# A decoder layer with attention and a state scan: the far groups' values by Strassen's scheme, with x's sums made by adding transfers, an earlier scan, and quad operands issued ahead of reads

## Chip, cores and metric

The kernel runs on one core of one Trainium2 chip. The time is that of the device for one execution, in microseconds (us): the median of three runs. A profile of one further execution shows what each engine did: PE is TensorE (matmuls), PEld its weight loads, DVE VectorE, ACT ScalarE, POOL GpSimd, SP SyncE. POOL and SP do little but issue DMA transfers.

## The reference, cut to what matters

One layer on x of 512 tokens by 1024 channels, in float32:

```python
proj = x @ w_in            # q | k | v (3 dilation groups x 8 heads x 64 each) | u (512) | gate logits (2 x 1024)
q, k = apply_rope(q, pos), apply_rope(k, pos)
for g, (window, dilation) in enumerate(((128, 1), (512, 4), (2048, 16))):
    o_g, lse_g = dilated_group_attention(q[:, :, g], k[:, :, g], v[:, :, g], window, dilation)
...
y_attn = attn @ w_attn_br                       # the groups' outputs weighted by softmax of lse
y_s = s5_ssm(u, ...)                            # complex diagonal state scan: h' = a h + b u, y = Re(c h) + d u
glu = gelu(y_s) @ w_glu
y_ssm = (glu[..., :512] * sigmoid(glu[..., 512:])) @ w_ssm_br
mixed = gates[..., 0, :] * y_attn + gates[..., 1, :] * y_ssm
h = layer_norm(alpha * x + mixed @ w_out)
x = layer_norm(alpha * h + (silu(h @ w_ff_gate) * (h @ w_ff_up)) @ w_ff_down)
```

The change concerns v of the groups 1 and 2 (the "far" values, 512 tokens by 2 x 512 columns, over 1024 channels), and the order of the scan's and the attention's work around it.

## The kernel before

**Precision.** Every float32 factor is held as a high part, rounded to the format that the matmul takes, and a low part, the rest. A product is three matmuls (high by high, low by high, high by low), accumulated in PSUM.

**Weights.** The 128 x 2048 blocks of `w_in` are fetched by SP, 1 MB each (two raw buffers). Each is split in two halves of 128 x 1024: ACT casts the high part (line 201), DVE subtracts it from the raw weights to get the low part (line 202). The parts go to one of three slots (class `Weights`). When a step's matmuls have been issued, `release` gives its slot back and issues the next split.

**Steps.** The list STEPS (line 35) gives the stages of the projection. A step is 24 matmuls of 128 x 128 by 512 tokens (lines 208 to 210), that is 8 pieces of 128 channels with 3 matmuls each. The steps are u (0 to 3), v of group 0 (4 to 7), gate logits (8 to 19), k of group 0 (20 to 23), q of group 0 (24 to 27), and the far values (28 to 35, `pv`). From step 36 on come five quads: the far q and k pairs (`QUADS` 0 to 3) and the last gate logits. A quad is a 2 x 2 block product by Strassen's scheme: seven products, each of 24 matmuls of 256 columns (line 1148), on sums of weight blocks (made by DVE in place, tile `rq`) and sums of x. `prepare_quad` issues sums, cast and subtraction for a product's operand; `quad_evict` reads the banks x, y and z when a product has completed what they hold: ACT copies into `qsnap` (line 1181), DVE adds and applies the rotation. Behind the quads follow the GLU, the branch projections, the output projection and the feed-forward part, which the change leaves as they are except for the order of PSUM banks.

**x's sums.** Strassen's x operands (`x23`, `x4` and one overwriting a quarter of `x_hi`, `x_lo`) are made from x in another order of tokens, fetched by POOL (`xf`, 2 x 1 MB). DVE makes four sums (`sums_x`), ACT and DVE split them (`split_x`). All this lies at steps 30.6 to 34.2.

**The order around them.** Each engine takes its instructions strictly in the order in which they were issued. All other work is placed by a table written by hand: `at_step(n, f)` runs f when the steps have come to n; a whole or half number is the middle or the end of a step, quads count four steps each. The state scan is dealt out by `drip`, so many columns of elementwise operations each half step, to DVE (line 79). Its matmuls of y (`ssm_out`, lines 718 and 726) come in two rounds in the middle of the steps 28 and 29, each followed at once by ACT's copies out of `yt` (line 734), DVE's additions of `yc`, and the GELU. `turn_y` (step 30) turns the result by way of DRAM. SCORES and WEIGHTS place the attention of the far groups: scores (`s`, line 827), with masks and sums on DVE (line 838), and transposes of the weights (`t`, line 850).

Of the kernel before, what the change touches and what calls it, by code (L numbers as in the profile page):

```python
# [16 lines left out]
P = 128  # L17
# [81 lines left out]
class Weights:  # L99
# [65 lines left out]

    def release(self):
        slot = self.held.popleft()
        if slot[0] is None and not self.extra_ok():
            return
        self.free.append(slot)  # L170
        self.split()


def emit(ctx, tc, i, out):
# [530 lines left out]
    def ssm_out(rnd):  # L705

        if rnd == 0:
            late.take(1000)
            ssm["ysb"] = gat(0, "ysb").rearrange("p (a i b c) -> p a i b c", a=2, i=4, b=2)
        ut, h, y = ssm["ut"], ssm["h"], ssm["ysb"]  # L710
        tb, cb = ([ring_(f"y{n}{rnd}{e}").rearrange("p (o i c) -> p o i c", o=2, i=2) for e in range(2)]
                  for ring_, n in ((scores, "t"), (turned, "c")))
        for e in range(2):
            for par in range(2):
                for half, rows in halves64:
                    for x, cols in halves64:
                        i_ = 4 * rnd + 2 * e + x
                        pe.matmul(tb[half][cols, par, e], ssm["tm"][rows, 2 * i_ + par, :], ut[rows, 2 * i_ + par, :],
                                  start=True, stop=True)
        for e in range(2):  # L720
            for half in range(2):
                for r in range(2):
                    for par, rows in halves64:
                        for x, cols in halves64:
                            i_ = 4 * rnd + 2 * e + x
                            pe.matmul(cb[par][cols, half, e], caf[rows, i_, r, half, :], h[r][rows, 2 * i_ + half, :],
                                      start=(r == 0), stop=(r == 1))
        is_ = slice(2 * rnd, 2 * rnd + 2)
        yf = [y[:, half, is_].rearrange("p i b c -> p (i b c)") for half in range(2)]
        y2 = at.tile([P, 2, 512], F32, tag=("sw", "cq")[rnd], name=f"y2_{rnd}", bufs=1)  # L730
        y2 = [y2[:, half] for half in range(2)]
        for half in range(2):
            for par in range(2):
                act.copy(y[:, half, is_, par], tb[half][:, par])
# [119 lines left out]
    def attn_values(kind, hp):  # L854
# [148 lines left out]
    at_step(9.5, store_k)  # L1003
    for j in range(4):
# [1 line left out]
    at_step(13, blocks)  # L1006
    at_step(13, states)
    for rnd in range(2):
        at_step(28 + rnd, ssm_out, rnd)
    at_step(30, turn_y)  # L1010
    for kind in range(2):
        for j, n in enumerate(SCORES[kind]):
            if j > 0:
# [46 lines left out]
                6: [t23[n][:, 4:8] for n in range(2)], 7: [t23[n][:, 0:4] for n in range(2)]}  # L1060

    def fetch_x():
        for n, h in enumerate(("g0", 2)):
            forms_x[n] = home(h, f"xf{n}").rearrange("p (k t) -> p k t", k=KT)
            pool.dma_start(forms_x[n], i["xk"][n].rearrange("p (k t) -> p k t", k=KT))

    def sums_x(n):
        strassen_sums(forms_x[0], forms_x[1], n)

    def split_x(n):  # L1070
        h1, h2 = forms_x[0], forms_x[1]
        if n == 0:
            t23 = [home(h, f"x23{m}", F32R).rearrange("p (k t) -> p k t", k=KT) for h, m in ((5, "h"), (7, "l"))]
            t4 = home(8, "x4", F32R).rearrange("p (n k t) -> p n k t", n=2, k=4)
            forms_x["f"] = forms_of(xp, t23, [t4[:, m] for m in range(2)])
        hi, lo = forms_x["f"][(7, 6, 4, 5)[n]]
        split(hi, lo, (h2[:, 0:4], h2[:, 4:8], h1[:, 4:8], h1[:, 0:4])[n])

    at_step(30.6, fetch_x)
    for n in range(4):  # L1080
        at_step(32 + 0.4 * n, sums_x, n)
        at_step(33 + 0.4 * n, split_x, n)


    qr, qops, qbank, qsnap, qz = {}, {}, {}, {}, {}
# [40 lines left out]

        w.after = rest

    w.jobs[quad_first] = deque((lambda j=j, n=n: prepare_quad(j, n)) for j in range(len(QUADS)) for n in QPREP)
    w.loads[quad_first] = deque((lambda b=b: load_quad(0, b)) for b in (0, 2))  # L1130
    qnext = deque(j for j in range(len(QUADS)) for n in QORDER)
    X_HOMES = ("g0", "g0", 1, 4, 4)

    def quad_bank(j, key):
        return bank({"x": 2 * (j % 2), "y": 2 - 2 * (j % 2), "z": 1}[key], f"q{key}{j}")

    def quad_product(j, n):
        key = {1: "x", 6: "x", 7: "x", 4: "x", 2: "y", 5: "z", 3: "z"}[n]
# [776 lines left out]
```

## Time and profile before

| | us |
|---|---|
| median of 3 runs (823.75 to 824.73) | 824.17 |
| the profiled execution | 825.21 |
| its span, first to last instruction | 823.4 |
| steps 28 to 35 with two y rounds and the first far scores (165.97 to 219.68) | 53.71 |
| the five quads and the attention between them (219.68 to 357.23) | 137.55 |
| from there to the tail | 446.27 |

The profile records every instruction of one execution. "Busy" is the time in which an engine ran at least one. Matmuls overlap in the records: how fast they follow each other is seen in their starts, not in their lengths. A bracket behind a row gives how long the engine idled before it, and which instruction or transfer released it. The window rows that the prediction shows give the busy time of each engine in one stretch of the span, with the granted clock of PE (1.00 is full speed). In nearly the whole span PE is busy; its idle time in the stages above is below 2 us each.

### The profile page before, as it was taken

The page shows a single profiled execution, that of the slowest core. Times are in us where ns is not written, and L with a number is a line of the kernel's source. Part 1 is how long each engine was busy: PE and PEld are TensorE (multiplying, and loading weights), DVE is VectorE, ACT ScalarE, POOL GpSimd, SP SyncE. Part 2 cuts the span into 40 slices and gives each one's busy share as a digit, 9 for nine tenths or more (in the row PEclk, how much of TensorE's full clock was granted, in tenths as well). Part 3 has the DMA queues.
Part 4 walks back from the last instruction along what each step waited for, and adds up shares of the span by engine and source line. Part 5 has one row for each costly group of instructions (what it writes and reads, how often), then busy time and mean ns, then how long its engine had stood idle before and what let it go on. Part 6 is the DMA issues. An engine that isn't in the chain of part 4 may idle for free.

```text
span 823.4 us, 13781 instructions
## 1 busy us (share of the span) xinstructions
PE 810.5 (98%) x5608; PEld 726.7 (88%) x5608; DVE 653.4 (79%) x1043; ACT 402.7 (49%) x597; POOL 76.3 (9%) x94
## 2 busy tenths in 40 slices
PE   9999999999999999999999999999999999999995
PEld 7888888888899999988888899999999999888884
DVE  6985899663888889755986699877777789789986
ACT  5964321245557625775333246555555545555520
POOL 0000001310002331100000320000000000020104
PEclk9999999999999999999999999999999999999998
DMA  8733435756226635652615134333323333674453
GB/s 338 189 113 127 159 139 145 154 129 205 78 78 140 138 91 122 181 216 93 252 55 205 51 123 169 119 107 106 106 109 112 115 111 111 273 168 149 147 132 102
DMA packets 31471, 116.43 MB, mean 141 GB/s; under 512 B 7600, under 2 KB 12464, under 8 KB 21680
## 3 DMA queue, kind: packets, MB, share of 16 engines
q1 hardware_dynamic: 23808, 91.83, 32.2%
q0 software_dynamic: 5968, 22.02, 12.4%
q10 hardware_dynamic: 1632, 1.70, 0.6%
q8 instruction: 44, 0.72, 0.3%
q14 instruction: 19, 0.16, 0.1%
HBM read 99.55 MB, written 9.70 MB: 133 GB/s over the span
## 4 chain that ended last, share of the span: by engine, by line
PE 92%; DVE 3%; DMA 1%; ACT 1%; POOL 1%; issue 1%; DVEq 0%; SPq 0%; ACTq 0%
PE qx L1148 5%; PE dnx L1672 5%; PE dnz L1672 4%; PE pg L208 3%; PE pg L209 3%; PE pg L210 3%; PE pv L208 3%; PE qz L1148 2%; PE pv L209 2%; PE pv L210 2%; PE pu L607 2%; PE dny L1672 2%; PE qy L1148 2%; PE wo L210 2%; PE wo L209 2%; PE b L210 2%
## 5 line engine op out<-in xcount | busy, mean ns | idle before, releaser
L202 DVE TENSOR_TENSOR wlo<-raw,whi 128x1024 fp32r<-128x1024 f32 x52 | 63.8, 1231 | 32.0 <-ACT whi L201 32.0
L201 ACT CAST whi<-raw 128x1024 fp32r<-128x1024 f32 x52 | 54.2, 1046 | 41.4 <-PE pq L209 17.5
L1472 ACT CAST whi<-sums 128x1024 fp32r<-128x1024 f32 x40 | 42.0, 1049 | 66.2 <-DVE sums L342 66.2
L1119 ACT CAST whi_q<-rq 128x1024 fp32r<-128x1024 f32 x28 | 29.2, 1051 | 42.1 <-DVE rq L342 42.1
L342 DVE TENSOR_TENSOR wlo<-sums,whi 128x1024 fp32r<-128x1024 f32 x40 | 48.8, 1220 | 0.0
L342 DVE TENSOR_TENSOR wlo_q<-rq,whi_q 128x1024 fp32r<-128x1024 f32 x28 | 34.1, 1222 | 12.9 <-ACT whi_q L1119 12.8
L1672 PE MATMUL dnx<-whi_d,pc 128*128 128x512 f32 (+1 forms) x128 | 38.2, 376 | 0.0
L208 PE MATMUL pg<-x_hi,whi 128*128 128x512 f32 x96 | 37.6, 392 | 0.0
L209 PE MATMUL pg<-x_lo,whi 128*128 128x512 f32 x96 | 37.4, 389 | 0.0
L840 ACT ACTIVATE un<-un,st 128x256 f32<-128x256 f32 (+1 forms) x64 | 30.8, 483 | 13.4 <-DVE st L838 13.4
L210 PE MATMUL pg<-x_hi,wlo 128*128 128x512 f32 x96 | 37.4, 389 | 0.0
L765 POOL DMA_DIRECT2D kq<-qz x32 | 25.2, 1315 | 108.9 <-PE s L827 48.1
L955 ACT ACTIVATE gt<-pg,bgate 128x512 f32<-128x512 f32 x12 | 8.3, 690 | 42.5 <-PE pg L210 42.5
L1584 ACT CAST whi_d<-dn 128x1024 fp32r<-128x1024 f32 x16 | 16.9, 1053 | 22.8 <-DVE dn L342 10.8
L1672 PEld LDWEIGHTS dnx<-whi_d,pc 128*128 128x128 f32 x128 | 23.6, 188 | 4.4
L208 PE MATMUL pv<-whi,x_hi 128*128 128x512 f32 x64 | 25.4, 397 | 0.0
L209 PE MATMUL pv<-wlo,x_hi 128*128 128x512 f32 x64 | 25.0, 390 | 0.0
L210 PE MATMUL pv<-whi,x_lo 128*128 128x512 f32 x64 | 24.9, 389 | 0.0
L342 DVE TENSOR_TENSOR wlo<-ra,whi 128x1024 fp32r<-128x1024 f32 x20 | 24.4, 1220 | 0.4 <-ACT whi L1472 0.4
L1594 POOL DMA_DIRECT2D whi_db<-in_w_dp x3 | 1.7, 576 | 246.1 <-PE dny L1672 242.4
L1672 PE MATMUL dnx<-wlo_d,pc 128*128 128x512 f32 (+1 forms) x64 | 24.1, 376 | 0.0
L1148 PE MATMUL qx<-x23h,whi_q 128*128 128x256 f32 x80 | 23.2, 290 | 0.7 <-ACT qsnap L1181 0.7
(800 smaller groups left out, 2939.2 us busy)
## 6 DMA issues: line engine op xcount, KB each, us to landing
raw<-in_w_in SPq DMA_DIRECT2D x16, 1024.0 KB, 4.9
ra<-in_w_gu SPq DMA_DIRECT2D x10, 1024.0 KB, 4.7
rb<-in_w_gu SPq DMA_DIRECT2D x10, 1024.0 KB, 4.9
rq<-in_w_quad SPq DMA_DIRECT2D x16, 512.0 KB, 4.0
dn<-in_w_dq SPq DMA_DIRECT2D x8, 1024.0 KB, 4.8
kq<-qz POOLq DMA_DIRECT2D x32, 128.0 KB, 5.4
raw<-in_w_br SPq DMA_DIRECT2D x4, 1024.0 KB, 4.7
raw<-in_w_out SPq DMA_DIRECT2D x4, 1024.0 KB, 4.8
```

The source lines that it names most:

```text
L201: act.copy(hi, src)
L202: dve.tensor_tensor(lo, src, hi.bitcast(F32), op=ALU.subtract)
L208: pe.matmul(dst, a[0], b[0], start=first, stop=False)
L209: pe.matmul(dst, a[0], b[1], start=False, stop=False)
L210: pe.matmul(dst, a[1], b[0], start=False, stop=last)
L342: eng.tensor_tensor(o, a, b, op=op)
L765: pool.dma_start(dst[32 * q : 32 * q + 32], z[32 * (q ^ 1) : 32 * (q ^ 1) + 32], accum_op=ALU.add)
L840: act.activation(pt, pt, AF.Exp, bias=mneg, scale=-1.0, accum_out=zsum)
L1119: act.copy(hi, src)
L1148: pe.matmul(d[:, 256 * e : 256 * e + 256], p_[:, e, k, :], q_[:, k, :], start=(first and e == k == m == 0), stop=(k == 3 and m == 2), skip ...
L1472: act.copy(hi, src)
L1672: pe.matmul(acc[key][0 if key == "v" else e][:, cs], p_, q_[:, cs], start=(key, e) not in begun, stop=(m == 2), skip_group_check=True)
```

## The change

**Far values.** The eight steps become one 2 x 2 block product (two halves of tokens; two halves of the 1024 channels; group 1 and group 2 columns) in seven products by Strassen's scheme. Each has two halves u of 12 matmuls with 512 columns. x's operands are stationary here and the weights stream. Three pairs of banks accumulate: x (0, 7), y (1, 2), z (5, 6). Product 4 starts banks 0 and 7 afresh, after products 1, 6 and 7 have been read out.

```diff
-STEPS += [("v", _g, _un, _c) for _g in (1, 2) for _un in range(2) for _c in range(2)]
+    VORDER = (1, 2, 5, 6, 3, 7, 4)
...
+    def prepare_v():
+        n, u = vleft.popleft()
+        a11, a12, a21, a22 = (vraw[b][:, 1024 * u : 1024 * u + 1024] for b in range(4))
+        hi, lo = w.take_slot(f"v{n}{u}")
+        vslot[n, u] = w.held.pop()
+        vops[n, u] = tuple(z.rearrange("p (k c) -> p k c", k=2) for z in (hi, lo))
+        two_steps({1: a11, 2: a12, 5: a21, 6: a11, 3: a12, 7: a21, 4: a22}[n], hi, lo)
+        if n == 5:
+            tt(a11, a21, a11, ALU.subtract)
+        elif n == 6:
+            tt(a12, a12, a11, ALU.subtract)
+        elif n == 3:
+            tt(a21, a22, a11, ALU.subtract)
...
+    def sum_v(u):
+        tt(*(vraw[b][:, 1024 * u : 1024 * u + 1024] for b in (2, 2, 3)), ALU.add)
...
+    def v_product(n, u):
+        key = {1: "x", 6: "x", 7: "x", 4: "x", 2: "y", 5: "z", 3: "z"}[n]
+        first = n in (1, 2, 5) and u == 0
+        if first:
+            vbank[key] = [bank(b, f"v{key}{b}") for b in {"x": (0, 7), "y": (1, 2), "z": (5, 6)}[key]]
+        ws, xs = vops.pop((n, u)), forms_x["f"][n]
+        for e in range(2):
+            for kk in range(2):
+                for m, (p_, q_) in enumerate(((0, 0), (0, 1), (1, 0))):
+                    pe.matmul(vbank[key][e], xs[p_][:, 2 * u + kk, 128 * e : 128 * e + 128], ws[q_][:, kk, :],
+                              start=(first and kk == m == 0), stop=(kk == 1 and m == 2), skip_group_check=True)
...
+            if n == 1:
+                act.copy(dst(1, 0), x)
+            elif n == 2:
+                tt(dst(1, 0), dst(1, 0), y, ALU.add)
...
+            elif n == 7:
+                tt(dst(2, 1), dst(2, 1), x, ALU.add)
+            else:
+                act.copy(dst(2, 0), x)
...
+    for n, m in enumerate(VORDER):
+        for u in range(2):
+            now = VQ_AT + 8 * (n + u / 2) / 7
...
+            v_product(m, u)
+            if u == 1:
+                v_evict(m)
+            w.held.appendleft(vslot.pop((m, u)))
+            w.release()
```

The two raw blocks of group 2 are fetched early into homes of their own (steps 19.5 and 22.6). Two more slots, made of tiles that are free at that time, let the weight halves be split further ahead.

**x's sums.** POOL fetches two halves of 512 KB at step 23. Each sum is a negation by ACT and a transfer on POOL's queue that adds the other half from DRAM:

```diff
-    def sums_x(n):
-        strassen_sums(forms_x[0], forms_x[1], n)
+    def sum_x(n):
+        h1, h2 = forms_x[0], forms_x[1]
+        dst, src, add = ((h1[:, 0:4], h1[:, 0:4], xk(1, 0)), (h2[:, 0:4], h2[:, 0:4], xk(1, 1)),
+                         (h2[:, 4:8], h1[:, 0:4], xk(1, 1)), (h1[:, 4:8], h2[:, 4:8], xk(0, 1)))[n]
+        act.mul(dst, src, -1.0)
+        pool.dma_start(dst, add, accum_op=ALU.add)
...
-    at_step(30.6, fetch_x)
-    for n in range(4):
-        at_step(32 + 0.4 * n, sums_x, n)
-        at_step(33 + 0.4 * n, split_x, n)
+    at_step(23, fetch_x)
+    at_step(24.4, sum_x, 0)
+    at_step(24.4, sum_x, 1)
+    at_step(24.9, swap_homes)
+    at_step(25.9, sum_x, 2)
+    at_step(27.4, sum_x, 3)
+    for n, at_ in enumerate((28.1, 27.2, 28.6, 29.6)):
+        at_step(at_, split_x, n)
```

**Order.** The scan, the y rounds and the first far scores move. `ssm_out` keeps its matmuls in the middle of a step; its second part, now `ssm_gelu` with ACT's copies, DVE's additions and the GELU, comes after the step's end. In a quad, the release of a slot (which issues the next operand's sum, cast and subtraction) comes ahead of the reads of the product's bank, and the banks x and y change places.

```diff
-SCORES = [[30, 36.3, 39.1, 41.9, 44.7], [49.5, 52.5, 54, 55.7, 58.2]]
-WEIGHTS = [[32, 38.1, 40.9, 43.7], [51, 53.2, 55, 57.2]]
+SCORES = [[33.8, 36.3, 39.1, 41.9, 44.7], [49.9, 52.5, 54, 55.7, 58.2]]
+WEIGHTS = [[35.2, 38.1, 40.9, 43.7], [51, 53.2, 55, 57.2]]
...
-    drip(9, 20, 1600)
-    drip(20, 28, 500)
+    drip(9, 20, 1850)
+    drip(20, 22, 1000)
...
-            at_step(7.5 + r, state_inputs, r, m)
-    at_step(9, scan)
+            at_step(7 + r, state_inputs, r, m)
+    at_step(8.9, scan)
...
-        at_step(28 + rnd, ssm_out, rnd)
-    at_step(30, turn_y)
+        at_step(22 + rnd, ssm_out, rnd)
+        at_step(22.5 + rnd, ssm_gelu, rnd)
+    at_step(24.5, turn_y)
...
-        return bank({"x": 2 * (j % 2), "y": 2 - 2 * (j % 2), "z": 1}[key], f"q{key}{j}")
+        return bank({"x": 2 - 2 * (j % 2), "y": 2 * (j % 2), "z": 1}[key], f"q{key}{j}")
...
             quad_product(j, n)
-            quad_evict(j, n)
             w.held.appendleft(qslot.pop((j, n)))
             w.release()
+            quad_evict(j, n)
...
-    glu, brs = ring(2, 1, 0), ring(0, 1, 2, 3)
+    glu, brs = ring(0, 1, 2), ring(2, 3, 0, 1)
```

What this moves in the engines' queues is shown at three places. A row is an instruction: its line (of the kernel it belongs to), its operation, what it writes and reads, and the shape.

The first is DVE in the changed kernel at the end of the far values. `wlo2_v40` and `wx_v41` are the low halves for product 4, `wlo0_q01` that of the first quad operand, `s` the scores of group 1, `vx0` and `vx7` the banks that product 7 has completed and that product 4 starts afresh.

```order
L349 TENSOR_TENSOR wlo2_v40_1965<-rv3_1526,whi2_v40_1964 128x1024
L349 TENSOR_TENSOR wx_v41_1982<-rv3_1526,wx_v41_1982 128x1024
L349 TENSOR_TENSOR wlo0_q01_1998<-rq0_1914,whi0_q01_1997 128x1024
L848 ISA un000_2014,st0_257<-s0000_2002,masks_131 128x128
...
L848 ISA un003_2029,st0_257<-s0021_2009,masks_131 128x256
L848 ISA st0_257 128x1
L349 TENSOR_TENSOR v2_1801<-v2_1801,vx0_1802 128x512
L349 TENSOR_TENSOR v2_1801<-v2_1801,vx7_1803 128x512
```

The additions of banks 0 and 7 stand behind three low halves and the eight score operations; before, there were no such additions.

The second is ACT at the first y round, before and in the changed kernel. `yt` are the banks of the y matmuls; `whi` with a number is a weight half, by its step.

```order
L201 CAST whi0_28_1538<-raw14_1435 128x1024
L201 CAST whi1_29_1570<-raw14_1435 128x1024
L201 CAST whi2_30_1607<-raw15_1505 128x1024
L734 COPY ysb_1628<-yt00_1629 128x2x128 x2
L734 COPY ysb_1628<-yt01_1630 128x2x128 x2
L737 ACTIVATE y2_0_1681<-ysb_1628 128x512 x2
L741 ACTIVATE y2_0_1681<-y2_0_1681 128x512 x2
L201 CAST whi0_31_1712<-raw15_1505 128x1024
```

```order
L201 CAST whi1_23_1363<-raw11_1224 128x1024
L201 CAST whi2_24_1401<-raw12_1295 128x1024
L201 CAST whi0_25_1487<-raw12_1295 128x1024
L744 COPY ysb_1418<-yt00_1419 128x2x128 x2
L744 COPY ysb_1418<-yt01_1420 128x2x128 x2
L747 ACTIVATE y2_00_1493<-ysb_1418 128x512
```

Before, the copies out of step 28's round come ahead of the cast for step 31, whose slot step 28 frees. Now the copies of step 22's round come behind the cast for step 25, whose slot step 22 frees at its end.

The third is DVE where the third quad (group 2's first, number 2) ends and the next begins, before and in the changed kernel: `rq` are raw weights and sums made in them, `wlo` and `wx` low halves of quad operands (`q36` is the quad 3, product 6), `qsnap` and the two lines with `rope` behind it the reads of a bank.

```order
L342 TENSOR_TENSOR wlo0_q35_2945<-rq1_1987,whi0_q35_2944 128x1024
L342 TENSOR_TENSOR qsnap_2121<-qsnap_2121,qz2_2806 128x512
L342 TENSOR_TENSOR kq20_2907<-qsnap_2121,rope_130 128x2x256
L342 TENSOR_TENSOR qz20_2908<-qsnap_2121,rope_130 128x2x256
L342 TENSOR_TENSOR rq1_1987<-rq1_1987,rq0_1893 128x1024
L342 TENSOR_TENSOR kq20_2907<-qx2_2770,rope_130 128x2x256
L342 TENSOR_TENSOR qz21_2940<-qx2_2770,rope_130 128x2x256
L342 TENSOR_TENSOR wlo1_q36_2982<-rq1_1987,whi1_q36_2981 128x1024
```

```order
L349 TENSOR_TENSOR wlo1_q35_2954<-rq1_1916,whi1_q35_2953 128x1024
L349 TENSOR_TENSOR rq1_1916<-rq1_1916,rq0_1914 128x1024
L349 TENSOR_TENSOR qsnap_2140<-qsnap_2140,qz2_2819 128x512
L349 TENSOR_TENSOR kq20_2924<-qsnap_2140,rope_130 128x2x256
L349 TENSOR_TENSOR qz20_2925<-qsnap_2140,rope_130 128x2x256
L349 TENSOR_TENSOR wlo2_q36_2988<-rq1_1916,whi2_q36_2987 128x1024
L349 TENSOR_TENSOR kq20_2924<-qx2_2783,rope_130 128x2x256
L349 TENSOR_TENSOR qz21_2958<-qx2_2783,rope_130 128x2x256
```

The sum for product 6 of the next quad now stands ahead of the three operations that read product 3's bank, and its low half ahead of the last two.

More of the change, by code (lines that the diff above doesn't have):

```diff
@@ L167, in release @@
         slot = self.held.popleft()
-        if slot[0] is None and not self.extra_ok():
+        if slot[0] is None and not self.extra_ok(slot[1]):
             return
@@ L240, in home, with swap_homes @@
     def home(n, name, dt=F32):
+        n = swapped.get(n, n)
         return gat(n[1:], name, dt) if isinstance(n, str) else big(n, name, dt)
+    swapped = {}
+    def swap_homes():
+        for a, b in ((2, 5), ("g0", 7), (6, 8)):
+            swapped[a], swapped[b] = b, a
     w = Weights(nc, wp, split)
@@ L727, in ssm_out, with ssm_gelu @@
                                       start=(r == 0), stop=(r == 1))
+        ssm["yb"] = tb, cb
+    def ssm_gelu(rnd):
+        y, (tb, cb) = ssm["ysb"], ssm["yb"]
         is_ = slice(2 * rnd, 2 * rnd + 2)
         yf = [y[:, half, is_].rearrange("p i b c -> p (i b c)") for half in range(2)]
-        y2 = at.tile([P, 2, 512], F32, tag=("sw", "cq")[rnd], name=f"y2_{rnd}", bufs=1)
-        y2 = [y2[:, half] for half in range(2)]
+        y2 = [at.tile([P, 512], F32, tag="un", name=f"y2_{rnd}{half}", bufs=4) for half in range(2)]
         for half in range(2):
@@ new lines, in split_x, with two_steps, plain_x @@
+        hi, lo = forms_x["f"][(5, 6, 7, 4)[n]]
+        src = (h1[:, 0:4], h2[:, 4:8], h2[:, 0:4], h1[:, 4:8])[n]
+        two_steps(src, hi, lo)
+    def two_steps(src, hi, lo):
+        act.copy(hi, src)
+        w.flush()
+        w.after = lambda: tt(lo, src, hi.bitcast(F32), ALU.subtract)
+    def plain_x():
+        half = [slice(0, 256), slice(256, 512)]
+        forms_x["f"] = {m: [xp[n][k][:, :, half[h]] for n in range(2)] for m, k, h in ((1, 0, 0), (2, 1, 0), (3, 1, 1), (5, 0, 1))}
+    plain_x()
@@ new lines, in sum_v, with more_slots @@
+    def sum_v(u):
+        tt(*(vraw[b][:, 1024 * u : 1024 * u + 1024] for b in (2, 2, 3)), ALU.add)
+    for u in range(2):
+        at_step(24.6 + u, sum_v, u)
+    def more_slots():
+        w.extra, w.extra_ok = lambda name, j: home(("g3", 0)[j], name, F32R), lambda j: len(vleft) > 0 and j == 0
+        for j in range(2):
+            w.free.append((None, j))
+            w.split()
+    at_step(24.4, more_slots)
+    def v_product(n, u):
[9 more added lines that the diff above has]
+                              start=(first and kk == m == 0), stop=(kk == 1 and m == 2), skip_group_check=True)
@@ new lines, in v_evict @@
+    def v_evict(n):
+        for e in range(2):
+            dst = lambda g, h: vs[g][:, 2 * h + e, :]
+            x, y, z = (vbank[k][e] if k in vbank else None for k in "xyz")
+            if n == 1:
+                act.copy(dst(1, 0), x)
+            elif n == 2:
+                tt(dst(1, 0), dst(1, 0), y, ALU.add)
+            elif n == 5:
+                act.copy(dst(2, 1), z)
+            elif n == 6:
+                act.copy(dst(1, 1), x)
+            elif n == 3:
+                tt(dst(1, 1), dst(1, 1), z, ALU.add)
+            elif n == 7:
+                tt(dst(2, 1), dst(2, 1), x, ALU.add)
+            else:
+                act.copy(dst(2, 0), x)
@@ L1131, in emit @@
+    for b, h in ((2, 5), (3, 7)):
+        at_step((19.5, 22.6)[b - 2], lambda b=b, h=h: load_v(b, home(h, f"rv{b}")))
+    w.jobs[quad_first] = deque([prepare_v] * len(vleft))
+    w.jobs[quad_first].extend((lambda j=j, n=n: prepare_quad(j, n)) for j in range(len(QUADS)) for n in QPREP)
+    w.loads[quad_first] = deque((lambda b=b: load_v_raw(b)) for b in range(2))
     qnext = deque(j for j in range(len(QUADS)) for n in QORDER)
@@ L1220, in emit, with extra @@
         run_fill(n + 0.5)
-    def extra(name):
+    w.flush()
+    for g in (1, 2):
+        vs[g] = home((3, "g1", 0)[g], f"v{g}").rearrange("p (b c) -> p b c", b=4)
+    for n, m in enumerate(VORDER):
+        for u in range(2):
+            now = VQ_AT + 8 * (n + u / 2) / 7
+            if any(k <= now for k in fill):
+                w.flush()
+            run_fill(now)
+            v_product(m, u)
+            if u == 1:
+                v_evict(m)
+            w.held.appendleft(vslot.pop((m, u)))
+            w.release()
+    def extra(name, _):
         return home(X_HOMES[w.extra_quad], name, F32R)
@@ L1231, in emit @@
             if (j, m) == (0, 0):
-                w.extra, w.extra_ok = extra, lambda: len(qnext) > 3
+                w.extra, w.extra_ok = extra, lambda _: len(qnext) > 3
+                assert all(p is not None for p, _ in w.free)
                 w.free.append((None, 0))
```

32 lines of the change are left out of this document (20 added, 12 removed).

## The prediction, made before the changed kernel ran

> **What bounds the kernel now.** I read the page's busy times first, then the chain of work that ended last, then the windows of the stages that the change touches.
>
> ```profile
> PE 810.5 (98%) x5608; PEld 726.7 (88%) x5608; DVE 653.4 (79%) x1043; ACT 402.7 (49%) x597; POOL 76.3 (9%) x94
> PE 92%; DVE 3%; DMA 1%; ACT 1%; POOL 1%; issue 1%; DVEq 0%; SPq 0%; ACTq 0%
> ```
>
> TensorE (PE) is busy for 98% of the span and carries 92% of the chain; the other steps of the chain are small. So a matmul taken away shortens the kernel by its full pace, as long as no other engine becomes late. The windows say where there is idle time to win. They are, in order: the far values with the two y rounds before them, the five quads, everything up to the tail, and the tail.
>
> ```profile
> core 0: us, PE busy (x) PEld busy (x) DVE busy (x) ACT busy (x) POOL busy (x), PEclk, DMA share, GB/s
> 165.97:219.68 53.71, 53.28 (x415) 43.62 (x414) 32.33 (x54) 27.99 (x54) 4.60 (x6) 1.00 0.48 143
> 219.68:357.23 137.55, 135.87 (x1251) 130.38 (x1252) 111.71 (x201) 81.73 (x182) 27.55 (x36) 1.00 0.52 132
> 357.23:803.50 446.27, 446.27 (x2923) 407.47 (x2922) 359.83 (x406) 216.34 (x271) 22.65 (x24) 1.00 0.40 135
> ```
>
> From 357.23 to 803.5 us PE has no gap at all and its granted clock is 1.00: the change leaves that stage's arithmetic alone, so I expect nothing of it. The far values (53.7 us) leave 0.4 us idle, the quads 1.7 us. VectorE (DVE) is busy for 32.3 of 53.7 us in the far values, and for 111.7 of 137.6 us in the quads, where it is the next bound.
>
> **1. Fewer matmuls.** Far values now take 8 steps x 24 = 192 matmuls of 512 columns; the changed kernel takes 7 products x 2 halves x 12 = 168 of the same size. One record lasts 389 to 397 ns, but records overlap, so the pace is read from start to start:
>
> ```profile
> 165.97 0.39 PE L208 MATMUL pv<-whi,x_hi 128*128 128x512 f32 x1
> 168.47 0.39 PE L210 MATMUL pv<-whi,x_lo 128*128 128x512 f32 x1
> ```
>
> These are the first and last of 12 matmuls: 11 gaps in 2.50 us, 0.227 us each. 24 fewer are **-5.45 us** (by the records' length it would be 9.3, which is wrong). Which operand is stationary has changed, not the shape, so I keep the pace. A full step of 24 is 5.45 us, a unit of 12 (one product's half) 2.72 us.
>
> **2. The passage from values to quads.**
>
> ```profile
> 218.87 0.39 PE L210 MATMUL pv<-whi,x_lo 128*128 128x512 f32 x1
> 219.68 0.39 PE L1148 MATMUL qx<-x_hi,whi_q 128*128 128x256 f32 x1 [0.43 <-ACT v L799]
> ```
>
> The gap is 0.81 us where the pace is 0.23: the first quad needs the bank that the last value step has just left to be copied. In the changed kernel the quad starts in bank 2, which the values finished with after product 2. **-0.58 us.**
>
> **3. Quad operands before reads.** Releasing a slot now issues the next operand's sum, cast and subtraction ahead of the reads of the product's bank. The trace has this stall:
>
> ```profile
> 303.99 0.28 PE L1148 MATMUL qz<-x_hi,wlo_q 128*128 128x256 f32 x1
> 305.00 0.38 PE L1148 MATMUL qx<-x23h,whi_q 128*128 128x256 f32 x1 [0.74 <-ACT qsnap L1181]
> 302.47 1.99 ACT L1119 CAST whi_q<-rq 128x1024 fp32r<-128x1024 f32 x2 [4.43 <-DVE rq L342]
> 304.37 0.58 ACT L1181 COPY qsnap<-qx 128x512 f32<-128x512 f32 x1
> 299.22 0.68 DVE L342 TENSOR_TENSOR qsnap<-qsnap,qz 128x512 f32<-128x512 f32 x1
> 301.14 1.22 DVE L342 TENSOR_TENSOR rq<-rq,rq 128x1024 f32<-128x1024 f32 x1
> 309.51 1.71 PE L827 MATMUL s<-kq 64*128 64x128 f32 x25 [0.73 <-DMA kq<-qz]
> ```
>
> PE lost 305.00 - 303.99 - 0.12 (the pace of 256 columns, half of 0.23) = 0.89 us. The copy it waited for stood behind two casts, the casts behind a DVE sum at 301.14, and the sum behind three reads that began at 299.22. In the new order the sum comes ahead of those reads, 1.92 us earlier. One more cast, half of 1.99 us, now stands ahead of the copy, so it ends about 0.9 us sooner: the stall goes, just. The second stall (bracket 0.73; the bracket of the first reads 0.15 below its starts, so 0.88) is the first scores of group 2, waiting for a transfer that the same DVE chain feeds. They are also moved back by one product (24 x 0.12 = 2.88 us). Together **-1.8 us**. What is late next is the copy itself. Smaller gaps exist:
>
> ```profile
> 292.33 0.28 PE L1148 MATMUL qz<-x_lo,whi_q 128*128 128x256 f32 x1
> 292.74 0.38 PE L1148 MATMUL qz<-x_hi,wlo_q 128*128 128x256 f32 x1
> ```
>
> That is 0.41 - 0.12 = 0.29 us; four such gaps, an estimate, would bring the gain to -3.0. The other end: if the added cast delays a copy and nothing is won, +1.0. I take the named stalls, since they have rows.
>
> **4. A new wait from product 7 to product 4.** Both accumulate in banks 0 and 7 in turn, and product 4 starts them afresh, so it must wait until DVE has added product 7 to the far values. In DVE's queue that addition stands behind the low half of the first quad operand (whose slot is freed only by product 7's first half, time T) and behind the eight score operations that now begin between the halves.
>
> ```profile
> 185.76 1.79 PE L827 MATMUL s<-kq 64*128 64x128 f32 x16
> 187.48 0.50 PE L208 MATMUL pv<-whi,x_hi 128*128 128x512 f32 x1
> 186.72 0.29 DVE L838 CUSTOM_DVE_ANT_0 un<-s,masks 128x128 f32<-128x128 f32 x1
> 189.21 0.08 DVE L838 DVE_READ_ACCUMULATOR2_ANT st<- 128x1 f32 x1
> 175.99 1.04 ACT L201 CAST whi<-raw 128x1024 fp32r<-128x1024 f32 x1
> 206.48 1.22 DVE L202 TENSOR_TENSOR wlo<-raw,whi 128x1024 fp32r<-128x1024 f32 x1
> 207.62 1.22 DVE L342 TENSOR_TENSOR xf<-xf 128x1024 f32<-128x1024 f32 x1
> ```
>
> PE reaches product 4 at T + 1.72 (scores, 185.76 to 187.48) + 2.72 = T + 4.4. DVE: cast 1.04 and its handover 0.2, low half 1.14 (206.48 to 207.62), scores 2.5 (186.72 to 189.21), the addition 0.68 (the row at 299.22): T + 5.6. **+1.1 us**; 0 if the low half is waited for less, 2 if DVE comes to it a full operation late.
>
> **5. A new wait in the second y round.** The y matmuls still stand in the middle of a step, but the reads of their banks now come after that step's end, behind a weight split and a rotation of k. The rows of before:
>
> ```profile
> 168.79 1.10 PE L718 MATMUL yt<-ut,tm 64*64 64x128 f32 x32
> 169.71 1.93 PE L726 MATMUL yc<-hst,ca 64*64 64x128 f32 x64
> 169.92 1.20 ACT L734 COPY ysb<-yt 128x256 f32<-128x256 f32 x4 [2.92 <-PE yt L718]
> 171.74 1.42 DVE L342 TENSOR_TENSOR ysb<-ysb,yc 128x256 f32<-128x256 f32 x4 [2.50 <-PE yc L726]
> 149.85 1.10 DVE L342 TENSOR_TENSOR kq<-pq,rope 128x512 f32<-128x512 f32 x1 [0.72 <-PE pq L210]
> 151.69 1.23 DVE L202 TENSOR_TENSOR wlo<-raw,whi 128x1024 fp32r<-128x1024 f32 x1
> ```
>
> From step 22's end E, DVE rotates for 1.84 us (149.85 to 151.69), splits for 1.14, then adds for 1.42: E + 4.4. (ACT's cast and copies are done at E + 2.2.) PE is at the second round's yc after half a step and yt: E + 2.72 + 0.92 (168.79 to 169.71) = E + 3.6. **+0.8 us**, between 0 (rotation not behind the step) and 1.2 (a late start of the rotation).
>
> **6. Costed at nothing: x's sums.** Four DVE sums become four ACT negations and four adding transfers of 512 KB on POOL's queue. The nearest rows are these:
>
> ```profile
> wlo_db<-in_w_dp POOLq DMA_DIRECT2D x3, 512.0 KB, 5.6
> raw<-in_w_in SPq DMA_DIRECT2D x16, 1024.0 KB, 4.9
> ```
>
> The first is an adding transfer of that size and queue. The sums start at steps 24.4, 25.9 and 27.4, that is 1.5 steps or 8.2 us apart, and each takes a negation (about 1.04, a cast's length) and 5.6. The tightest is sum 2: started 11.4 us ahead of the values (2.1 steps), wanted 5 us into them, so 16.4 us for 6.6. The cover is gone at about 11 us a transfer (below).
>
> [...]
>
> **7. Costed at nothing: the scan and the y rounds moved ahead.** DVE carries the scan between the splits:
>
> ```profile
> core 0: us, DVE busy (x), PEclk, DMA share, GB/s
> 62.00:146.20 84.20, 50.13 (x109) 1.00 0.43 141
> 62.00:146.20 84.20, 17.09 (x14) 1.00 0.43 141
> ```
>
> The first row is the scan's line, the second the splits': 67.2 of 84.2 us. The scan must now be done by step 22, six steps sooner, so it is dealt out faster: 1850 columns every half step, where an operation counts as its 256 columns and 100 more. That is 6 operations, 12 a step (1600 gave 5, so 10).
>
> ```profile
> 77.05 0.88 DVE L79 TENSOR_TENSOR sst<-sst,prep 128x256 f32<-128x256 f32 x2
> 80.80 1.22 DVE L202 TENSOR_TENSOR wlo<-raw,whi 128x1024 fp32r<-128x1024 f32 x1
> ```
>
> Ten operations stand between these two starts, 0.375 us each. So a step of 5.45 us gets 12 x 0.375 + 1.14 = 5.64 us of DVE work: DVE falls behind by 0.2 a step, some 2 us over the ten steps of the scan. By the starts of these operations I find 2.7 us in hand before PE would wait for step 22's low half. If this cover is gone, PE waits for what is missing.
>
> **Sum.** -5.45 - 0.58 - 1.8 + 1.1 + 0.8 = -5.9 on the profiled execution of 825.2 us (span 823.4): 819.3. The median of the three runs, 824.17, lies 1.04 below the profiled one, so **818.2 us**. By the terms' ends: -9.0 (815.1) and -1.8 (822.3).
>
> **Rivals.**
> - *Values wait for operands* (chance 0.18). Weight halves pass through five slots. For it: the stage has 14 low halves, 6 weight sums and 4 low halves of x, 24 x 1.14 = 27.4 us of DVE, with six additions (0.68) and the scores 34 in some 42 us (7 x 5.45, 1.72 of scores, some 2 of transposes), all in order; by my walk x form 5 and product 6 have only some 1 us in hand. Against: DVE has 8 us free. Price: two or three waits of 1 to 1.5 us, +3: about 821.
> - *The quad stalls stay* (0.12). The extra cast ahead of the copy eats what the earlier sum wins. Term 3 is 0: 820.0.
> - *All stalls go* (0.12): terms 4 and 5 vanish because DVE is ahead, and term 3 is -3: 815.1.
> - *The change does not take out what it says* (0.04): a switch of stationary operands at every unit, 14 x 0.1 to 0.2 us, and the waits above, +3 to 4: about 822.5, no change.
> - *Slower: the adding transfers* (0.06). The chain is fetch, negation, sum 0, negation, sum 2, negation, sum 3; ACT's queue is in order, so a late landing holds the weight casts behind it. Decides from 11 us a transfer on, about twice the 5.6 of the row. At 12 us, product 5's and product 6's operands are some 6.4 and 4.4 us late: 818.2 + 10.8 = 829.
> - My own case holds the remaining 0.48.
>
> **Chances and range.** 0.2% (1.65 us) is about what a measurement of this kernel can tell from no change: faster is below 822.5. My case, the quads' rival, the better one and four fifths of the operand rival lie there: 0.48 + 0.12 + 0.12 + 0.14 = 0.86. Slower is the transfers' 0.06, the rest 0.08 the same. The range 814.8 to 822.4 takes in the ends of the terms and leaves out the two last rivals and the tails.
>
> **What would show it.** The far values' stage should last about 7 x 5.45 + scores and transposes; its matmul starts 0.227 apart, and one wait of about 1 us on the additions of far values, ahead of product 4. The second y round should show a wait of some 0.8 us on the reads of the first. The waits of quad matmuls on ACT's snapshot and on the transfer of kq should be gone. From the first unit after the quads on, every distance should be as before. Wrong would be waits on a weight's low half or on an x form in the values, adding transfers near 11 us, a value matmul pace above 0.23, or waits in steps 15 to 22.

## The result, and the profile after

The changed kernel takes **832.63 us** (median of 4 runs, 830.25 to 835.46); the kernel before takes 824.42 (4 runs, 823.75 to 824.73). The ratio is 1.0102, 95% interval 1.007 to 1.0135: it is slower by 1%, where 818.2 us and "faster" had been forecast. The profiled execution took 832.69 us, 7.48 more than that of before (825.21). One execution of all those below, of e9 (879.51 us, at a granted clock of 0.849), was in a slow state and is left out of its median.

First the page of the changed kernel (busy times, the chain that ended last), then its windows, in the columns of before: the far values, the quads, all up to the tail.

```profile
PE 807.5 (97%) x5584; PEld 724.5 (87%) x5584; DVE 667.8 (80%) x1059; ACT 412.5 (50%) x607; POOL 80.2 (10%) x98
PE 89%; DVE 3%; DMA 3%; ACT 2%; SPq 1%; POOL 1%; issue 1%; DVEq 0%; ACTq 0%
```

```profile
core 0: us, PE busy (x) PEld busy (x) DVE busy (x) ACT busy (x) POOL busy (x), PEclk, DMA share, GB/s
173.39:230.11 56.72, 45.23 (x200) 36.03 (x198) 38.49 (x51) 28.41 (x45) 5.31 (x6) 0.88 0.39 88
230.11:364.29 134.18, 133.76 (x1252) 129.94 (x1251) 109.11 (x199) 83.05 (x184) 27.61 (x36) 1.00 0.54 134
364.29:811.01 446.72, 446.72 (x2925) 407.89 (x2924) 359.43 (x407) 215.50 (x270) 23.06 (x25) 1.00 0.40 135
```

PE has fewer matmuls and is busy for 3.0 us less, but its share of the chain has fallen from 92% to 89%. The last stage is as before (446.72 against 446.27 us), the quads are 3.4 us shorter, and the far values are where the time goes: 11.5 of 56.7 us idle, at a mean clock of 0.88. Before, that stage had 53.71 us with the two y rounds in it (2 x 2.78), so 48.15 without them: it has grown by 8.6.

The list of what PE waited for names the place. Columns: who waited for whom, us in total, times, the longest.

```profile
PE vz L1214 <- DVE x_lo L349: 9.3, 1, 9.3
PE vz L1214 <- ACT x_hi L1100: 1.3, 1, 1.3
...
PE vx L1214 <- ACT un L850: 0.9, 1, 0.9
PE yc L733 <- DVE ysb L349: 0.5, 1, 0.5
```

Both large waits stand at the start of product 5 (bank z): it waits first for the high part of x form 5, then 9.3 us for its low part. The two below them are the waits that the prediction had named. Now the timelines of DVE, ACT and SP's queue ahead of that place (start, length, instruction, idle time before it and releaser).

```profile
179.63 1.22 DVE L349 TENSOR_TENSOR wlo_v<-rv,whi_v 128x1024 fp32r<-128x1024 f32 x1
191.08 1.23 DVE L349 TENSOR_TENSOR x23l<-xf,x23h 128x1024 fp32r<-128x1024 f32 x1 [10.23 <-DMA ydr<-ysb]
...
194.49 1.22 DVE L349 TENSOR_TENSOR x_lo<-xf,x_hi 128x1024 fp32r<-128x1024 f32 x1
```

```profile
173.28 1.05 ACT L1100 CAST whi_v<-rv 128x1024 fp32r<-128x1024 f32 x1 [9.42 <-DMA rv<-in_w_in]
174.24 1.05 ACT L1085 ACTIVATE xf<-xf 128x1024 f32<-128x1024 f32 x1
...
181.83 1.05 ACT L1100 CAST x23h<-xf 128x1024 fp32r<-128x1024 f32 x1 [4.65 <-DMA xf<-in_xk]
```

```profile
162.90 0.33 SPq L1169 DMA_DIRECT2D rv<-in_w_in  x1
163.28 22.18 SPq L761 DMA_DIRECT2D ydr<-ysb  x16
```

DVE stands still for 10.2 us, in order, ahead of `x23l`, the low part of form 6. For the last 8.2 of them the data that it needs are there: ACT's cast of the high part ends at 182.88 (181.83 + 1.05). It waits because `x23l` is written into the home (`gat0`, a piece of on-chip memory that several tiles use in turn) from which `ydr<-ysb`, the 16 transfers of the y turn, are still reading. `x_lo`, for which PE waits, is the third operation behind it (191.08 to 194.49). ACT loses 9.4 us on the weight block `rv` and can begin the negation for sum 2 (at 174.24) only behind it. These are all transfers of one crowd:

```profile
rv<-in_w_in SPq DMA_DIRECT2D x1, 1024.0 KB, 10.3
xf<-in_xk POOLq DMA_DIRECT2D x4, 512.0 KB, 6.3
ydr<-ysb SPq DMA_DIRECT2D x16, 64.0 KB, 7.6
```

The last column is the median time from issue to landing. The blocks took 4.9 us before; the 16 transfers took 2.1, at 185 to 196 us, where the DMA engines were taken for 0.50 of the time (103 GB/s).

### The profile page after: what moved, and what is told of

It reads as the page before. It is cut to its first block, busy times and chain, and to the rows that moved or that the text cites. A ratio compares the mean times of both kernels' runs of the same rounds, so it can differ in the third digit from the quotient of the medians.

```text
span 830.9 us, 13774 instructions
## 1 busy us (share of the span) xinstructions
PE 807.5 (97%) x5584; PEld 724.5 (87%) x5584; DVE 667.8 (80%) x1059; ACT 412.5 (50%) x607; POOL 80.2 (10%) x98
## 4 chain that ended last, share of the span: by engine, by line
PE 89%; DVE 3%; DMA 3%; ACT 2%; SPq 1%; POOL 1%; issue 1%; DVEq 0%; ACTq 0%
PE qx L1258 7%; PE dnx L1798 5%; PE dnz L1798 4%; PE qz L1258 3%; PE pu L614 3%; PE pg L208 3%; PE pg L210 3%; PE pg L209 3%; PE dny L1798 2%; DMA ydr<-ysb 2%; PE wo L210 2%; PE wo L208 2%; PE b L208 2%; PE b L210 2%; PE b L209 2%; PE wo L209 2%
## 5 line engine op out<-in xcount | busy, mean ns | idle before, releaser
L202 DVE TENSOR_TENSOR wlo<-raw,whi 128x1024 fp32r<-128x1024 f32 x44 | 54.2, 1235 | 17.7 <-ACT whi L201 17.7
L201 ACT CAST whi<-raw 128x1024 fp32r<-128x1024 f32 x44 | 45.9, 1048 | 22.9 <-PE pk L209 17.4
L1258 PE MATMUL qz<-x_hi,whi_q 128*128 128x256 f32 x80 | 22.8, 286 | 0.0
L1258 PE MATMUL qz<-x_hi,wlo_q 128*128 128x256 f32 x80 | 22.6, 283 | 0.0
L1258 PE MATMUL qz<-x_lo,whi_q 128*128 128x256 f32 x80 | 22.6, 283 | 0.0
```

The source lines that it names most:

```text
L201: act.copy(hi, src)
L202: dve.tensor_tensor(lo, src, hi.bitcast(F32), op=ALU.subtract)
L1258: pe.matmul(d[:, 256 * e : 256 * e + 256], p_[:, e, k, :], q_[:, k, :], start=(first and e == k == m == 0), stop=(k == 3 and m == 2), skip ...
```

## The experiments

Each ratio is to the kernel before as it ran beside the experiment (medians 824.38 to 824.70).

**The home, alone (e1).** The low part of forms 6 and 7 goes to another home, x form 4, which is split later, to the one of `ysb`:

```diff
-            t23 = [home(h, f"x23{m}", F32R).rearrange("p (k t) -> p k t", k=KT) for h, m in ((5, "h"), (7, "l"))]
-            t4 = home(8, "x4", F32R).rearrange("p (n k t) -> p n k t", n=2, k=4)
+            t23 = [home(h, f"x23{m}", F32R).rearrange("p (k t) -> p k t", k=KT) for h, m in ((5, "h"), (8, "l"))]
...
+        if n == 3:
+            t4 = home(7, "x4", F32R).rearrange("p (n k t) -> p n k t", n=2, k=4)
...
-    for n, at_ in enumerate((28.1, 27.2, 28.6, 29.6)):
+    for n, at_ in enumerate((28.1, 27.2, 28.6, 31.6)):
```

> The changed kernel with x23l and x4 in exchanged homes, and the split of x form 4 moved from step 29.6 to 31.6; the y turn and the adding transfers stay. Theory (VectorE stands still because x23l is written into the home that the 16 transfers ydr<-ysb are still reading): VectorE's wait of 10.2 us on ydr is gone, product 5's lost time falls from 12.5 us to some 1.5, product 2's 1.5 us stay; 822 to 824 us. Rival (the adding transfers are late by themselves, and ydr only happens to land at the same time): x's low half still comes about 190 us into the span, product 5 loses 8 us or more, 829 to 831 us.

Measured: 824.81 us (10 runs; ratio to before 0.9999, 0.9987 to 1.0012), 7.8 less than the change and 0.8 above the range of its theory, and DVE no longer waits for `ydr`. So the home, with what is still reading from it, is about half of the 14 us that product 5 lost. (The profiled execution of e1, 826.54 us, is one of its longer ones, and the rows below are from it.) (What the expectations here call product 2's 1.5 us is the wait for form 5's high part, between product 2's last matmul and product 5's first.) That wait did not stay at 1.3 us:

```profile
188.06 0.50 PE L1216 MATMUL vz<-whi_v,x_hi 128*128 128x512 f32 x1 [4.26 <-ACT x_hi L1102]
188.39 0.40 PE L1216 MATMUL vz<-wlo_v,x_hi 128*128 128x512 f32 x1
189.88 0.79 PE L1216 MATMUL vz<-whi_v,x_lo 128*128 128x512 f32 x1 [1.09 <-DVE x_lo L349]
```

ACT reaches `x_hi` only behind the cast of sum 2, and `rv` landed after 11.3 us in this run. So time is lost in this stretch beside the home as well.

**The y turn later (e2).** As e1, with one line:

```diff
-    at_step(24.5, turn_y)
+    at_step(30.6, turn_y)
```

> As e1, and the y turn (16 transfers ydr<-ysb on SP's queue) at step 30.6 instead of 24.5. Theory (beside the home, these transfers crowd the weight block rv and the adding transfers): rv lands in 5 to 7 us instead of 10.3, ScalarE does not stand before it for 9.4 us, sum 2 starts some 4 us sooner, and the far values lose nothing but the wait ahead of product 4; 818 to 820 us. Rival (the crowding is the adding transfers' own): rv still takes 10 us, product 2 still loses 1.5 us, as e1, 822 to 824 us.

Measured: 824.00 us (10 runs; 0.9989, 0.9975 to 1.0003), e1 within the spread of either. The edit did not do what it was for:

```profile
L761 SPq DMA_DIRECT2D ydr<-ysb x16: 302/562/2468, 163.1 to 182.6; - x16
```

The transfers are issued from 163.1 us on, as in the change (163.3). SP's queue has nothing between the block `rv` and the quads' weights, so a later place in the program is the same place in its queue, and SP issued them at the same time. The run says nothing on the theory.

**x's sums on DVE (e3).** Whole fetches, and the sums of before at the steps of the change; homes and turn as changed:

```diff
-            pool.dma_start(forms_x[n][:, 0:4], xk(n, 0))
+            pool.dma_start(forms_x[n], i["xk"][n].rearrange("p (k t) -> p k t", k=KT))
...
-        act.mul(dst, src, -1.0)
-        pool.dma_start(dst, add, accum_op=ALU.add)
+        strassen_sums(forms_x[0], forms_x[1], n)
```

> The changed kernel with x's four sums made by VectorE from two whole 1 MB fetches, at the same steps; homes and y turn as changed. Theory (home of ysb): VectorE still waits on ydr<-ysb ahead of x23l; with less traffic the transfers end perhaps sooner, so product 5 loses 3 to 12 us, 824 to 832 us. Rival (the sums' transfers are the cause): no wait of VectorE on ydr above 2 us, 819 to 821 us.

Measured: 821.99 us (4 runs; 0.996, 0.9947 to 0.9974). DVE does not wait for `ydr` at all, although it still writes into `ysb`'s home: without the adding transfers the 16 land in time. The theory in its first form, the home alone, falls; the rival's 819 to 821 is missed by 1 us.

```profile
rv<-in_w_in SPq DMA_DIRECT2D x1, 1024.0 KB, 5.6
ydr<-ysb SPq DMA_DIRECT2D x16, 64.0 KB, 4.1
```

**What crowds: the turn's small pieces (e6) or the adding (e7)?** e6 writes the turn in 4 transfers of whole rows; e7 lets the four sum transfers copy, which leaves the sums out:

```diff
-        for x in range(2):
-            for j in range(4):
...
-                    sp.dma_start(yv[x][j][:, :, par], ysb[r0 : r0 + 16, :, par])
+        for x in range(4):
+            sp.dma_start(yv[:, x], ysb[:, x])
```

> The changed kernel; the y turn writes ysb to DRAM in 4 transfers of whole 2 KB rows instead of 16 transposing ones (y's order is then wrong, so the output is; bytes the same). Theory (the crowding comes from the 16 transposing transfers sharing the DMA engines with rv and the sums): rv lands in 6 to 7 us, ydr by 172, VectorE does not wait on it, 820 to 823 us. Rival (the adding transfers crowd by themselves): rv still takes 9 to 10 us, sum 2 starts no sooner than 174, product 5 still loses 4 us or more, 825 us or more.

```diff
-        pool.dma_start(dst, add, accum_op=ALU.add)
+        pool.dma_start(dst, add)
```

> The changed kernel; the four sum transfers copy instead of adding (x's sums are left out, so the output is wrong; transfers, bytes written and order are the same). Theory (adding, with its second read, is what makes these transfers crowd the others): sum 1 and rv land in 5 to 7 us, ydr before 182, 821 to 824 us. Rival (their bytes and the transposing transfers crowd, added or not): rv 9 to 10 us, VectorE's wait on ydr 8 us or more, 829 to 832 us.

Measured: e6 824.54 us (8 runs; 0.9999), e7 819.97 (2 runs; 0.994, 0.9922 to 0.9959). The windows from 161 to 191 us of the change, e3, e6 and e7, in this order (columns as above; the last two are the DMA engines' share and GB/s):

```profile
161.00:191.00 30.00, 24.16 (x106) 19.37 (x104) 16.67 (x16) 13.90 (x17) 10.58 (x12) 0.95 0.88 176
```
```profile
161.00:191.00 30.00, 28.19 (x118) 22.86 (x117) 29.97 (x30) 12.60 (x14) 6.85 (x8) 0.94 0.54 105
```
```profile
161.00:191.00 30.00, 26.33 (x110) 21.11 (x109) 23.41 (x23) 13.59 (x16) 10.48 (x12) 0.96 0.85 175
```
```profile
161.00:191.00 30.00, 28.89 (x128) 23.61 (x127) 26.38 (x26) 17.00 (x19) 9.35 (x12) 1.00 0.70 176
```

At the same rate (176 GB/s) the transfers hold the DMA engines for 0.88 of the time when they add and 0.70 when they copy; without them, at 105 GB/s, it is 0.54. In e7 DVE's wait for `ydr` is 1.3 us instead of 10.2, though `rv` still takes 9.4. In e6, with the turn's pieces gone and the bytes the same, `rv` takes 9.8 and sum 2 starts hardly sooner (174.67 against 175.59), yet the 4 transfers end at about 179 instead of 191, and DVE does not wait for them. So the 12.7 us between the change and e7 come from the adding: beside it the 16 transfers land in a median of 7.6 us and the last is issued at 184.6, without it these are 4.3 and 177.1; the four transfers themselves land in 6.3 and 4.6. `rv` hardly gains. The transposing pieces make it worse: e6 is 8.1 us below the change, between its two cases. Neither expectation of e7 holds in full: `rv` stayed slow, as its rival said, and the time fell even below what its theory gave. The second read that the theory names is seen in no trace.

**The quads' part, on the kernel before (e4).** Release ahead of the reads, the banks, and the first scores of group 2 at 49.9:

```diff
             quad_product(j, n)
-            quad_evict(j, n)
             w.held.appendleft(qslot.pop((j, n)))
             w.release()
+            quad_evict(j, n)
```

> The kernel before with only the quad part of the change: release ahead of the reads, banks x and y exchanged, first scores of group 2 at 49.9, and the rings of banks behind. Theory: both named stalls go (-1.8 us) and the passage from values to quads does not wait (-0.6): 821.8 us, to 822.4 if only one of them. Rival (the cast ahead of the copies eats it): 824.2 us, no change.

Measured: 823.42 us (11 runs; 0.9986, 0.9977 to 0.9995): faster, by 1.2 us of the 1.8 to 2.4. The quads' window shows the gain, the waits show what is left:

```profile
220.58:354.83 134.25, 133.85 (x1250) 130.03 (x1251) 110.87 (x201) 81.54 (x180) 27.62 (x36) 1.00 0.54 135
```
```profile
PE qx L1148 <- ACT v L799: 0.9, 1, 0.9
```

134.25 against 137.55 us: 3.3 in the quads, more than the two named stalls. In the profiled executions 2.4 us of it are left (822.83 against 825.21), by the medians 1.2. The wait for the copies of the far values, 0.43 before, is 0.9 here. The rows explain it: of the four copies in a row, the quad of before starts when the first is done (219.06 + 0.6; it starts at 219.68), that of e4, with the banks exchanged, when the last is (218.48 + 2.04 = 220.52; it starts at 220.58).

**DVE's order (e5), and the waits that had been forecast (e8).** e5 is e3 with form 5 split first and sum 3 later. e8 adds to it the y reads in the middle of the steps, as before, and product 4 in banks 1 and 2, with the quads' banks as before:

```diff
-    at_step(27.4, sum_x, 3)
-    for n, at_ in enumerate((28.1, 27.2, 28.6, 29.6)):
+    at_step(28.9, sum_x, 3)
+    for n, at_ in enumerate((28.1, 28.3, 28.6, 29.6)):
```

> As e3 (x's sums on VectorE), with form 5 of x split ahead of form 6 (28.1 and 28.3 instead of 28.1 and 27.2) and x sum 3 at step 28.9 instead of 27.4. Theory (what is left in the far values of e3 is VectorE's order alone: four operations ahead of x's low half that are wanted later): product 5's lost 3.75 us go, 818.3 us. Rival (VectorE has no room: the same work comes due at product 6 or 3 instead): the loss moves and 820.5 to 822 us are left.

```diff
-        at_step(22.5 + rnd, ssm_gelu, rnd)
+        at_step(22 + rnd, ssm_gelu, rnd)
...
-        key = {1: "x", 6: "x", 7: "x", 4: "x", 2: "y", 5: "z", 3: "z"}[n]
-        first = n in (1, 2, 5) and u == 0
+        key = {1: "x", 6: "x", 7: "x", 4: "y", 2: "y", 5: "z", 3: "z"}[n]
+        first = n in (1, 2, 5, 4) and u == 0
```

> As e5, and product 4 accumulates in banks 1 and 2 (free since product 2) with the quads' and later banks as before the change, and the reads of the y rounds stand in the middle of the steps, right behind the y matmuls, as before the change. Theory: the wait ahead of product 4 (0.9 by its bracket, 1.3 by starts) and that of the second y round (0.5 and 0.2 by brackets, 1.0 by starts) both go, 2 us below e5: 816.2 us. Rival (the time comes back, since VectorE is what paces the far values): as e5 within 0.5.

Measured: e5 820.34 us (5 runs; 0.9948, 0.9935 to 0.996), e8 816.13 (4 runs, 816.04 to 816.85; **0.9897, 0.9882 to 0.9912**). e5 fell between its two cases: product 5 loses nothing now, but product 6 waits 1.5 us for a low half. In e8 this is gone as well, and with it both waits that had been forecast. That e8 meets its 816.2 is partly luck: that was set 2 us below the 818.3 that e5 was to reach; e5 stayed at 820.34, and the drop was 4.2, of which product 6's wait, which had not been named, is 1.5. Why it went too was not taken apart.

```profile
PE 803.3 (99%) x5584; PEld 722.5 (89%) x5584; DVE 672.0 (83%) x1063; ACT 408.5 (50%) x603; POOL 76.5 (9%) x94
PE 95%; ACT 1%; DVE 1%; POOL 1%; issue 0%; DVEq 0%; ACTq 0%
```
```profile
172.21:213.91 41.70, 41.70 (x200) 34.18 (x199) 37.96 (x50) 24.00 (x39) 3.43 (x4) 1.00 0.30 77
```

The far values take 41.70 us without a wait: 7 x 5.45, the scores 1.72, the transposes 1.45, and 0.4 at the places where they change. DVE is busy for 38.0 of them. e8 beats both kernels: it is 8.6 us below the kernel before in its comparison.

**The price of the adding transfers in a kernel without the other waits (e9).** e8 with the transfers in place of DVE's sums, and e1's homes:

> As e8, but x's sums by the adding transfers, as in the change; x23l and x4 in exchanged homes as in e1 (form 4's split at 31.6, forms 5 and 6 at 28.1 and 28.3, sum 3 at 27.4). It prices the adding transfers in a kernel without the other waits. Theory (they crowd the weight block rv, and ScalarE, in order, stands before it): rv lands in 9 to 11 us instead of e8's 8.8 or less, after 171, product 2 loses 1 to 4 us and product 5 another 1 to 3; 819 to 823 us. Rival (once the home is exchanged and the order mended, the transfers find room): 816 to 817 us.

Measured: 821.21 us (median of 9 runs, 819.86 to 823.71; 0.9965, 0.9954 to 0.9976), 5.1 above e8. Product 5 starts late on both parts of its form:

```profile
PE vz L1216 <- ACT x_hi L1102: 1.4, 1, 1.4
...
PE vz L1216 <- DVE x_lo L349: 0.7, 1, 0.7
```

The time lies in the range of the theory, but the wait that the theory named is not the one that costs: ACT waits 8.8 us for `rv`, and in e8, where PE waits for nothing in the far values, it is 9.2 (`rv` takes 10.3 and 8.8 us). New in e9 is a wait for sum 2, ahead of the last negation, with `x_hi` behind it in ACT's order (at 176.13 in e8):

```profile
181.57 1.06 ACT L1085 ACTIVATE xf<-xf 128x1024 f32<-128x1024 f32 x1 [7.45 <-DMA xf<-in_xk]
183.47 1.04 ACT L1102 CAST x_hi<-xf 128x1024 fp32r<-128x1024 f32 x1
```

Sum 2 was issued at 172.52, so it took 9 us; the four transfers of this run land in a median of 11.0 us (6.0 to 14.9). The 5.1 us are the price of the whole path, negations on ACT included, and e9 also differs from e8 in the exchanged homes and in the places of sum 3 and of form 4's split.

## Why the prediction was wrong, step by step

| Step | forecast, us | measured, us | from |
|---|---|---|---|
| 1 fewer matmuls | -5.45 | -5.45 | 0.227 apart in products 1, 6, 3 and 7 |
| 2 passage to the quads | -0.58 | -0.6 | no wait; the quad starts 0.23 behind the last value matmul |
| 3 quads | -1.8 | -3.4 | windows, 137.55 to 134.18; in e4 -3.3 |
| 4 product 7 to 4 | +1.1 | +1.05 | rows below |
| 5 second y round | +0.8 | +1.0 | rows below |
| 6, 7 at nothing | 0 | +14.0 | product 5 |

The last is read from starts: product 5 lasts from 185.77 to 203.67, 17.90 us instead of 5.45, and its first matmul comes 1.5 us late. The sum of the column is +6.6; the measured difference of 7.5 has 0.9 more, most of it in stages whose matmuls the change leaves alone (0.4 behind the quads, 0.3 ahead of step 20).

The places of steps 4 and 5, on PE in the changed kernel:

```profile
221.72 0.39 PE L1214 MATMUL vx<-whi_v,x23l 128*128 128x512 f32 x1
223.00 0.47 PE L1214 MATMUL vx<-whi_v,x 128*128 128x512 f32 x1 [0.89 <-ACT un L850]
```
```profile
144.61 0.39 PE L210 MATMUL pk<-x_hi,wlo 128*128 128x512 f32 x1
144.93 1.10 PE L725 MATMUL yt<-ut,tm 64*64 64x128 f32 x32
146.53 2.29 PE L733 MATMUL yc<-hst,ca 64*64 64x128 f32 x64 [0.49 <-DVE ysb L349]
```

Product 4's start is 1.28 us after the matmul before it, 1.05 over the pace. The releaser named there is ACT's `un`; e8 shows that it is the bank, since the wait goes when product 4 uses another. The yc matmuls start 1.60 after yt (0.92 before) and, as the next matmul's start at 148.75 shows, take 2.22 from start to start where they took 1.86: 1.0 together.

**The step that failed is the one that cost the moves at nothing (6 and 7).** What step 7 counted, the scan's and the splits' operations on DVE, did cost nothing: after its warm-up PE waits for nothing until the second y round. But it counted none of the y turn's 16 transfers, which moved with the y rounds from 185 us to 163, into the very stretch where step 6 placed the adding transfers and where the weight block `rv` is fetched. Step 6 had the landing of a sum nearly right (a median of 6.3 us, 5.3 to 10.3, against 5.6) and asked only whether the sums themselves would be in time. It did not ask what they do to the transfers beside them, although the three adding transfers from which it took the 5.6 us show it in the kernel before: while they run, with copies and a weight block beside them, the DMA engines are taken for 0.86 of the time.

```profile
727.40:743.60 16.20, 16.20 (x73) 13.41 (x72) 12.82 (x13) 8.74 (x9) 3.19 (x4) 1.00 0.86 179
```

It did not ask whose home the sums' splits write to either. And sum 2, which was to start 11.4 us ahead of the values, began 0.9 us into them (its negation at 174.24, the values at 173.39), since on ACT it stands behind the cast that waited for `rv`. The chain of what happened: the sums add (0.88 of the DMA engines' time is taken), the turn's transfers land up to 191 us, DVE stops ahead of a tile that one of them still reads, and everything behind it in DVE's order is late. Product 5's wait on an x form is one of the signs of being wrong that the prediction had named.

e1 takes the home away (-7.8), e6 the small pieces (-8.1), e3 the adding transfers (-10.6), e7 only the adding (-12.7). After any one of them DVE's stop of 10.2 us is gone (1.3 are left in e7), so that stop needs home, pieces and adding together. What e1 and e6 still lose (in their profiles product 5 begins 4.4 and 2.7 us late) goes with the adding: in e7, which keeps home and pieces, product 5 begins on time.

The rival that ended slower, at 829 us, was given 0.06. It named the right transfers, but that it came near the time is luck, since its mechanism was another: it was to decide from 11 us a transfer, and no sum took longer than 10.3.

The rest held. Take the 14 us from the profiled 832.7 and 818.7 are left, beside the 819.3 of the sum; that they are so close is partly luck, since the 1.6 us that step 3 gained beyond its forecast and the 0.9 us that no step names cancel in part. Quad operands ahead of reads were mis-sized: 3.4 us, even beyond the lower end (-3.0), since the smaller gaps went too (quad matmuls that start 0.1 us or more late: 13 before, 2.5 us in all; 3 in the changed kernel, 0.3). Two figures of the forecast were estimates without a row: term 4's handover of 0.2 us from a cast to its low half (in the changed kernel the low half at 174.37 began 0.04 us after the cast at 173.28 had ended), and a rival's 0.1 to 0.2 us for each switch of stationary operands (in e8 all the places where the far values change take 0.4 us together).

## What to carry to other kernels

A transfer that is moved takes the tile that it reads and the DMA engines' time with it (here a stop of 10.2 us, and from 161 to 191 us engines that were taken for 0.88 of the time, 0.50 before): list what writes into that tile next, and which transfers share the stretch, before costing the move at nothing. A later place in the program did not delay the transfers of e2 (from 163.1 us; 163.3 in the change), since their queue had nothing ahead of them. Where an elementwise sum can be made on an engine that has room, that can be cheaper than an adding transfer, whose price is paid by the transfers beside it and by what waits for them: about 5 us between e8 and e9.

## What the hardware showed that was not expected

**An idle of 1.8 us cost about as much again.** After product 5's wait, PE's matmuls do not resume their pace:

```profile
186.11 0.40 PE L1214 MATMUL vz<-wlo_v,x_hi 128*128 128x512 f32 x1
195.76 0.80 PE L1214 MATMUL vz<-whi_v,x_lo 128*128 128x512 f32 x1 [9.26 <-DVE x_lo L349]
196.35 0.63 PE L1214 MATMUL vz<-whi_v,x_hi 128*128 128x512 f32 x1
196.78 0.63 PE L1214 MATMUL vz<-wlo_v,x_hi 128*128 128x512 f32 x1
```

From 196.35 on they are 0.427 apart, until 201.5, at a granted clock of 0.50; then 0.227 again, at 1.00 from 203.6 on. That is some 12 gaps of 0.2 us, 2.4 us in the 14. It takes much less than 9 us: in e3 the wait lasted 1.81 us, and the half pace began 1.35 us after the resumption and lasted for about 3 us (some 8 gaps of 0.2 us, 1.6 us).

```profile
186.54 0.50 PE L1210 MATMUL vz<-whi_v,x_lo 128*128 128x512 f32 x1 [1.81 <-DVE x_lo L349]
...
187.89 0.63 PE L1210 MATMUL vz<-wlo_v,x_hi 128*128 128x512 f32 x1
188.31 0.63 PE L1210 MATMUL vz<-whi_v,x_lo 128*128 128x512 f32 x1
```

In e5 a wait of 1.5 us left the pace (0.23) and the granted clock (1.00) as they were; in e9, with two waits of 1.4 and 0.7 us and two matmuls between them, the granted clock was a mean of 0.79 from 184.56 to 192.74. So among single waits 1.5 us did not halve the pace and 1.8 us did; that is one profile each, and what sets the half pace off is not shown. None of the forecast's prices for a wait of some microseconds had this part.
